# Joining the diagonal products of two token tiles into one planned operation in an encoder layer

## The chip, the cores and the metric

The kernel runs on one core of a Trainium2 chip. The metric is the device time of one execution in microseconds (us); lower is better. The engines are called TensorE (PE, with its weight loads as PEld), VectorE (DVE), ScalarE (ACT), GpSimd (POOL) and SyncE (SP, which here issues transfers).

## The reference

One layer of a bidirectional hybrid encoder on 512 tokens of width 1024, float32. One input projection feeds neighbourhood attention, a bidirectional state-space mixer (SSD) with 32 heads of width 64 in 8 groups, and gates; the branches are projected, merged and projected again, and a feed-forward layer follows. What matters here is the SSD mixer, which works in chunks of 128 tokens:

```python
def ssd_chunked(xh, dt, a, bmat, cmat):
    # xh (B,S,G,R,P), dt (B,S,G,R), a (G,R), bmat/cmat (B,S,G,N)
    ...
    a_cs = jnp.cumsum(adt, axis=-1)
    seg = a_cs[..., :, None] - a_cs[..., None, :]
    lmat = jnp.exp(jnp.where(tril, seg, -jnp.inf))
    cb = jnp.einsum('bclgn,bcsgn->bcgls', cc, bc)
    y_diag = jnp.einsum('bcgls,bcgrls,bcsgrp->bclgrp', cb, lmat, xc)
    states = jnp.einsum('bclgn,bcgrl,bclgrp->bcgrpn', bc, decay_states, xc)
    ...
    y_off = jnp.einsum('bclgn,bcgrpn,bcgrl->bclgrp', cc, prev, jnp.exp(a_cs))
    return (y_diag + y_off).reshape(bsz, s, g, r, p)
...
y_f = ssd_chunked(xs, dt[:, :, 0], a[0], bm, cm)
y_b = flip(ssd_chunked(flip(xs), flip(dt[:, :, 1]), a[1], flip(bm), flip(cm)))
y = y_f + y_b + xs * d_skip.astype(f32).reshape(SSD_GROUPS, HEADS_PER_GROUP)[..., None]
...
y = y * lax.rsqrt(jnp.mean(jnp.square(y), axis=-1, keepdims=True) + RMS_EPS)
y = y * ssd_norm_w.astype(f32).reshape(SSD_GROUPS, NORM_GROUP)
ys = y.reshape(bsz, s, D_INNER).astype(u.dtype) @ w_ssd_br
```

The change concerns `y_diag`, the products inside a chunk.

## The kernel before, in words

The first 485 us hold the input projection, the eight SSD groups and the projection of the SSD branch. Their instructions are not issued as the code is written: every step is first noted as an operation of a `Plan`, with its engine, a cost in us, the tile parts that it reads and writes, and whether it may fill gaps (`filler`, the long projections). A list scheduler then gives an order. The rank of an operation is its longest path to the end; `NUDGES`, a table of seeds and spreads, multiplies the ranks by small random factors, so each table gives another order. The start is written out by hand (`HEAD`, about the first 350 instructions of TensorE, to 58.9 us). `issue()` (L344) puts the hand-written start and the scheduled rest together, and `MOVE` there shifts one named operation ahead of another. Each engine then works its own queue in that order, and waits only for what its next instruction needs. Everything after the groups (attention, merge, feed-forward) has its order from the code.

For each group g, `ssd_project` makes four banks `ps_x` (B, C and two halves of x) by split products: `mm3` (L404 to L406) multiplies high times high, low times high and high times low parts, each 512 wide. `conv` copies each bank with a bias and a scale on ACT (L776), adds four taps on DVE (L784) and applies silu on ACT (L787), giving tiles `cv`. `z_project` makes `ps_z` the same way, 256 wide, and `sz` from it (L831). The weights of all of these come in slabs (`ws`), of which ACT makes the high half `wh` (L509) and POOL or DVE the low one `wl` (L513).

`ssd(g, ...)` then does, per group:

- `tp_b` (L858, transposes of B, which need `cv` of the first bank), `cb` (L868, the products of C and B, four token tiles in one bank), `tp_x` (L878) and `xtok` (L881), the weighted inputs `xw` (POOL, L913/L918), the chunk states `st` (L929, L941) and the states `hst`.
- For each half `c2` of the group, that is two token tiles `c`: one bank `yd` with room for both tiles. For each tile, a transfer brings the cumulated decays from DRAM (`acs_d`) to a tile `bc` (issued by SP at L959; there are 4 `bc` buffers). DVE and POOL subtract (L963), DVE makes a predicated copy (L967), ACT takes the exponent (L969), DVE multiplies by `cb` (L971). Then `f_yd` (L978) makes the diagonal products of that tile, 4 heads times 2 row halves, 64x64 each, which the profile shows as 16 instructions of form 128*64. So each half has two operations `f_yd`, each waiting for one `bc` and writing one half of the bank, and the planner may put them apart.
- `yo` (L993), the products across chunks, `t1`, `t2` and the sum `yz` (L1013).

`gated_norm(g, ...)` multiplies by `sz`, takes the sum of squares (ACT, L1028), finds the inverse root by 16 small operations on POOL (L1038 to L1056), scales the four tiles on ACT (L1059), and transposes on TensorE: two `tp_y` (L1075), from which ACT makes `yTh` (L1078) and DVE `yTl` (L1080). `ssd_branch` multiplies them by the slab `sbr` into eight banks `ps_sbr`, which are added up in `ysacc` (L1101; a copy for group 0).

Of the kernel before, what the change touches and what calls it, by code (L numbers as in the profile page):

```python
# [27 lines left out]
HD = 64  # L28
# [34 lines left out]

NUDGES = ((265225, 0.01), (410045, 0.001), (566648, 0.0005), (745606, 0.0005), (658272, 0.001), (17203, 0.0005),
          (943025, 0.0005), (429358, 0.001), (235890, 0.0005), (366213, 0.001))
LN0_BANKS = (("tr", "tr", "yd", "so"), ("tr", "tr", "yd", "tr"))
WDT = ("DVE", 0.66)
W0_ENG = lambda nc: (nc.gpsimd, nc.vector, nc.gpsimd, nc.vector)
# [36 lines left out]

MOVE = (("bc0_3.1", 2), ("bc0_2.0", 1))


class Plan:
# [233 lines left out]
    def issue(self):  # L343
        order = self.order(NUDGES)  # L344
        named = {}
        for o in self.ops:
            named.setdefault(".".join(map(str, o["w"][0])), []).append(o["i"])
        early, late = (named[x][n] for x, n in MOVE)
        head = [named[x[2:]].pop(0) for x in HEAD]
        order.remove(early)  # L350
        order.insert(order.index(late), early)
        done = set(head)
        for i in head + [i for i in order if i not in done]:
            self.ops[i]["fn"]()
# [3 lines left out]
def encoder_layer(ctx, tc, x, w_in, w_attn_br, w_ssd_br, w_o, w_ff1, w_ff2, pcols, rows64,  # L358
                  d_skip, ln_rows, rpb_pad, consts, lmask, out, dbg=None):
    nc = tc.nc  # L360
# [124 lines left out]
    op = plan.op  # L485

    def bank(name, tag, shape):
        return plan.tile(name, tag, psx, shape, F32)
# [36 lines left out]
    def load_x(t):  # L525
# [7 lines left out]
       r=[(xts[0].name, 0)], w=[(xts[2].name, 0), ("behind", 0)])  # L533
# [11 lines left out]
    for t in range(NT):  # L545
        for j in range(2):
# [3 lines left out]
           w=[("mv", t)])  # L550
# [298 lines left out]
    def ssd(g, bT, cT, x0, x1):  # L849
# [104 lines left out]
        for c2 in range(2):  # L954
            cs = slice(2 * c2, 2 * c2 + 2)
            yd = bank(f"yd{g}_{c2}", "yd", [P, 2, 256])
            for c in (2 * c2, 2 * c2 + 1):
                bc = local(f"bc{g}_{c}", "bc", [P, 2, HPG, P])
# [15 lines left out]

                def f_yd(c=c, bc=bc, yd=yd):
                    for h in range(HPG):
                        for rows in (slice(0, 64), slice(64, P)):
                            nc.tensor.matmul(yd()[rows, c % 2, h * HD : (h + 1) * HD],  # L978
                                             bc()[:, 1, h, rows],
                                             xtok()[:, c, h * HD : (h + 1) * HD], start=True, stop=True)  # L980
                op("PE", 0.9, f_yd, r=[(bc.name, 1), (xtok.name, c2)], w=[(yd.name, c % 2)])


# [828 lines left out]
```

## Time and profile before

| what | value |
| --- | --- |
| device time, median of 3 runs | 1178.44 us (1177.24 to 1178.65) |
| device time of the profiled execution | 1177.95 us |
| its span in the trace | 1176.2 us |
| mean granted clock of TensorE | 0.996 |
| busy time of TensorE | 1153.0 us, 98% of the span |

A row of the timeline reads: start in us, duration in us, engine, line, operation, the tile written and the tiles read, the shape, and the number of like instructions in a row; in square brackets the idle time of the engine just before, and what ended it. The start is that of the first of the row, the duration reaches to the end of the last. The matmuls overlap: each starts before the one ahead has ended, so their cost is read from start to start. Waits are given per line as total, number and longest.

### The profile page before, as it was taken

The page shows a single profiled execution, that of the slowest core. Times are in us where ns is not written, and L with a number is a line of the kernel's source. Part 1 is how long each engine was busy: PE and PEld are TensorE (multiplying, and loading weights), DVE is VectorE, ACT ScalarE, POOL GpSimd, SP SyncE. Part 2 cuts the span into 40 slices and gives each one's busy share as a digit, 9 for nine tenths or more (in the row PEclk, how much of TensorE's full clock was granted, in tenths as well). Part 3 has the DMA queues.
Part 4 walks back from the last instruction along what each step waited for, and adds up shares of the span by engine and source line. Part 5 has one row for each costly group of instructions (what it writes and reads, how often), then busy time and mean ns, then how long its engine had stood idle before and what let it go on. Part 6 is the DMA issues. An engine that isn't in the chain of part 4 may idle for free.

```text
span 1176.2 us, 16965 instructions
## 1 busy us (share of the span) xinstructions
PE 1153.0 (98%) x6394; PEld 977.1 (83%) x6394; DVE 765.4 (65%) x1363; ACT 614.9 (52%) x1033; POOL 545.5 (46%) x588
## 2 busy tenths in 40 slices
PE   5999999999999999999999999999999999999997
PEld 5988797879888888888888888888988888888886
DVE  7757476776766665434788975556543567498855
ACT  6677583836365554524667774342363554365410
POOL 1269968778788777204667630016046131221000
PEclk9999999999999999999999999999999999999999
DMA  6353333333333341233333313543236987888411
GB/s 202 98 161 124 108 126 108 125 106 129 108 108 111 123 144 59 85 108 86 93 78 89 77 47 108 179 156 131 73 108 192 239 202 189 188 214 224 151 65 54
DMA packets 129409, 149.22 MB, mean 127 GB/s; under 512 B 22960, under 2 KB 101808, under 8 KB 129328
## 3 DMA queue, kind: packets, MB, share of 16 engines
q1 hardware_dynamic: 115696, 112.63, 30.6%
q0 software_dynamic: 13056, 34.61, 12.2%
q8 instruction: 50, 0.82, 0.3%
q10 hardware_dynamic: 576, 0.92, 0.2%
q14 instruction: 31, 0.25, 0.1%
HBM read 145.90 MB, written 2.23 MB: 126 GB/s over the span
## 4 chain that ended last, share of the span: by engine, by line
PE 84%; DVE 5%; DMA 5%; issue 2%; ACT 2%; POOL 1%; SPq 1%; DVEq 0%; POOLq 0%; ACTq 0%
PE ps_f L404 8%; PE ps_f L406 8%; PE ps_f L405 8%; PE ps_x L404 4%; PE ps_x L406 4%; PE ps_x L405 4%; PE ps_abr L1370 4%; PE ps_z L404 3%; PE ps_z L405 3%; PE ps_z L406 3%; PE ps_sbr L404 2%; PE ps_sbr L406 2%; PE ps_sbr L405 2%; DMA w2r<-in_w_ff 2%; PE ps_g L405 2%; PE ps_g L404 2%
## 5 line engine op out<-in xcount | busy, mean ns | idle before, releaser
L784 DVE SCALAR_TENSOR_TENSOR cv<-ps_x,pc,cv 128x511 f32<-128x511 f32 (+1 forms) x128 | 95.7, 748 | 25.2 <-ACT cv L776 21.8
L405 PE MATMUL ps_f<-h1Th,wl_f 128*128 128x512 f32 (+1 forms) x288 | 104.1, 365 | 0.0
L404 PE MATMUL ps_f<-h1Th,wh_f 128*128 128x512 f32 (+1 forms) x288 | 103.6, 365 | 0.0
L406 PE MATMUL ps_f<-h1Tl,wh_f 128*128 128x512 f32 (+1 forms) x288 | 102.0, 365 | 0.0
L1573 DVE TENSOR_TENSOR wl_f<-w2r,wh_f 128x1024 fp32r<-128x1024 f32 x42 | 50.0, 1222 | 63.6 <-ACT wh_f L1572 63.3
L404 PE MATMUL ps_z<-wh_z,hTh 128*128 128x256 f32 x256 | 75.2, 294 | 0.0
L406 PE MATMUL ps_z<-wl_z,hTh 128*128 128x256 f32 x256 | 71.5, 279 | 0.0
L405 PE MATMUL ps_z<-wh_z,hTl 128*128 128x256 f32 x256 | 71.5, 279 | 0.0
L1567 POOL DMA_DIRECT2D w2r<-in_w_ff x30 | 36.3, 1415 | 72.5 <-DMA w2r<-in_w_ff 46.8
L405 PE MATMUL ps_f<-wh_f,sql 128*128 128x512 f32 x168 | 65.3, 390 | 0.0
L406 PE MATMUL ps_f<-wl_f,sqh 128*128 128x512 f32 x168 | 65.2, 390 | 0.1
L404 PE MATMUL ps_f<-wh_f,sqh 128*128 128x512 f32 x168 | 64.9, 389 | 0.0
L1572 ACT ACTIVATE wh_f<-w2r 128x1024 fp32r<-128x1024 f32 x42 | 42.7, 1054 | 42.0 <-DMA w2r<-in_w_ff 32.7
L1101 DVE TENSOR_TENSOR ysacc<-ps_sbr,ysacc 128x512 f32<-128x512 f32 x56 | 38.5, 689 | 37.5 <-PE ps_sbr L406 37.1
L404 PEld LDWEIGHTS ps_f<-h1Th,wh_f 128*128 128x128 f32 x288 | 53.9, 188 | 8.9
L405 PEld LDWEIGHTS ps_f<-h1Th,wl_f 128*128 128x128 f32 x288 | 53.9, 188 | 8.7
L406 PEld LDWEIGHTS ps_f<-h1Tl,wh_f 128*128 128x128 f32 x288 | 52.8, 188 | 8.7
L387 DVE TENSOR_TENSOR wl_f<-ws_f,wh_f 128x1024 fp32r<-128x1024 f32 x36 | 47.2, 1348 | 19.4 <-ACT wh_f L386 18.9
L404 PE MATMUL ps_x<-hTh,wh_bc 128*128 128x512 f32 (+1 forms) x144 | 56.6, 393 | 0.0
L404 PE MATMUL ps_sbr<-yTh,wh_sbr 128*128 128x512 f32 x128 | 55.8, 436 | 0.8 <-ACT yTh L1078 0.4
L406 PE MATMUL ps_x<-hTl,wh_bc 128*128 128x512 f32 (+1 forms) x144 | 53.5, 371 | 1.8 <-DVE hTl L626 1.8
L404 PE MATMUL ps_x<-hTh,wh_x 128*128 128x512 f32 (+1 forms) x144 | 54.6, 379 | 0.0
(344 smaller groups left out, 3717.0 us busy)
## 6 DMA issues: line engine op xcount, KB each, us to landing
ws_f<-in_w_ff SPq DMA_DIRECT2D x20, 1024.0 KB
w2r<-in_w_ff POOLq DMA_DIRECT2D x18, 1024.0 KB, 8.2
bc<-acs_d SPq DMA_DIRECT2D x32, 512.0 KB
w2r<-in_w_ff POOLq DMA_DIRECT2D x30, 512.0 KB, 8.9
ws_bc<-in_w_in SPq DMA_DIRECT2D x16, 512.0 KB
ws_x<-in_w_in SPq DMA_DIRECT2D x8, 1024.0 KB
ws_z<-in_w_in SPq DMA_DIRECT2D x8, 1024.0 KB
ws_g<-in_w_in SPq DMA_DIRECT2D x8, 1024.0 KB
```

What stands on the lines that cost most here:

```text
L387: (eng[i] if isinstance(eng, tuple) else eng).tensor_tensor(out=lo[:, k], in0=st[:, k], in1=hi[:, k].bitcast(F32), op=ALU.subtract)
L404: nc.tensor.matmul(o, lh, rh, start=start, stop=False)
L405: nc.tensor.matmul(o, ll, rh, start=False, stop=False)
L406: return nc.tensor.matmul(o, lh, rl, start=False, stop=stop)
L784: op("DVE", 0.75, lambda j=j, o=o, n=n: nc.vector.scalar_tensor_tensor(out=acc()[:, o], in0=ps()[:, n], scalar=tap(j), in1=acc()[:, o], op ...
L1101: op("DVE", 0.69, lambda d=d, ps=ps: nc.vector.tensor_tensor(out=ysacc[:, d, :], in0=ps(), in1=ysacc[:, d, :], op=ALU.add), r=[(ps.name, 0 ...
L1370: ins.append(nc.tensor.matmul(pss[j], u, v, start=k + p == 0, stop=k == KD - 1 and p == 2))
L1567: nc.gpsimd.dma_start(t, rows(i, n, c, k), accum_op=ALU.add)
L1572: nc.scalar.activation(hi[:, k], x, AF.Copy)
L1573: low = nc.vector.tensor_tensor(out=lo[:, k], in0=x, in1=hi[:, k].bitcast(F32), op=ALU.subtract)
```

## The change

The two `f_yd` of a half group become one operation. It is noted after both `bc` tiles are, with a cost of 1.2 us (`YD`) for the planner in place of two of 0.9, it reads both `bc` tiles and writes both halves of the bank. Its 16 matmuls of the program (32 in the profile) are the same ones in the same order as before within each tile. `MOVE` is dropped, with its use in `issue()`, and `NUDGES` is another table, of 14 entries in place of 10.

```diff
-NUDGES = ((265225, 0.01), (410045, 0.001), (566648, 0.0005), (745606, 0.0005), (658272, 0.001), (17203, 0.0005),
...
+NUDGES = ((169262, 0.0005), (921561, 0.003), (234225, 0.0005), (601575, 0.003), (892301, 0.001), (966086, 0.001), (247218, 0.001), (170282, 0.0005), (136193, 0.0005), (519613, 0.003), (845123, 0.0005), (776131, 0.001),
...
+YD = 1.2
...
-MOVE = (("bc0_3.1", 2), ("bc0_2.0", 1))
...
-        early, late = (named[x][n] for x, n in MOVE)
         head = [named[x[2:]].pop(0) for x in HEAD]
-        order.remove(early)
-        order.insert(order.index(late), early)
...
             yd = bank(f"yd{g}_{c2}", "yd", [P, 2, 256])
+            bcs = []
             for c in (2 * c2, 2 * c2 + 1):
                 bc = local(f"bc{g}_{c}", "bc", [P, 2, HPG, P])
...
-                def f_yd(c=c, bc=bc, yd=yd):
+                bcs.append(bc)
+
+            def f_yd(c2=c2, bcs=bcs, yd=yd):
+                for j, bc in enumerate(bcs):
                     for h in range(HPG):
                         for rows in (slice(0, 64), slice(64, P)):
-                            nc.tensor.matmul(yd()[rows, c % 2, h * HD : (h + 1) * HD],
-                                             bc()[:, 1, h, rows],
-                                             xtok()[:, c, h * HD : (h + 1) * HD], start=True, stop=True)
-                op("PE", 0.9, f_yd, r=[(bc.name, 1), (xtok.name, c2)], w=[(yd.name, c % 2)])
+                            nc.tensor.matmul(yd()[rows, j, h * HD : (h + 1) * HD], bc()[:, 1, h, rows],
+                                             xtok()[:, 2 * c2 + j, h * HD : (h + 1) * HD], start=True,
+                                             stop=True)
+            op("PE", YD, f_yd, r=[(bc.name, 1) for bc in bcs] + [(xtok.name, c2)],
+               w=[(yd.name, 0), (yd.name, 1)])
```

With the new table the whole order between 59 and 480 us is another one. The number of instructions on each engine is the same. Three places show how it differs; the numbers behind a name are the group, the tile or half, and a running number of the tile.

The first is TensorE in group 7, the second half of the diagonal products, before:

```order
L406 MATMUL ps_z7_1_4415<-wl_z7_4253,hTh_69 128x256
L978 MATMUL yd7_1_4447<-xtok7_4436,bc7_3_4143 64x64 x8
L929 MATMUL st7_03_4458<-xw7_3_4445,btok7_4259 128x256
L929 MATMUL st7_03_4458<-xw7_0_4456,btok7_4259 128x256
L978 MATMUL yd7_1_4447<-xtok7_4436,bc7_2_4133 64x64 x8
L404 MATMUL ps_z7_1_4415<-wh_z7_4238,hTh_69 128x256
```

And the same place now, TensorE in group 7:

```order
L404 MATMUL ps_z7_1_4415<-wl_z7_4252,hTh_69 128x256
L980 MATMUL yd7_1_4465<-xtok7_4454,bc7_2_4127 64x64 x8
L980 MATMUL yd7_1_4465<-xtok7_4454,bc7_3_3970 64x64 x8
L927 MATMUL st7_03_4486<-xw7_0_4482,btok7_4258 128x256
L927 MATMUL st7_03_4486<-xw7_3_4463,btok7_4258 128x256
L402 MATMUL ps_z7_1_4415<-wh_z7_4237,hTh_69 128x256
```

The two tiles now stand together, ahead of the `st` products that stood between them. Groups 3, 4 and 6 each had one half that was split in the same way; in group 0 and group 1 one half each had its two tiles far apart.

The second place is the end of group 0 on TensorE, where its transposes `tp_y0` meet the branch products `ps_sbr0`, before:

```order
L406 MATMUL ps_z1_1_1214<-wl_z1_1033,hTh_69 128x256
L1075 MATMUL tp_y0_1_1319<-cst_81,yz0_1093 128x128 x4
L1075 MATMUL tp_y0_0_1326<-cst_81,yz0_1093 128x128 x4
L929 MATMUL st1_03_1333<-xw1_0_1315,btok1_991 128x256
L929 MATMUL st1_03_1333<-xw1_3_1331,btok1_991 128x256
L404 MATMUL ps_sbr0_0_1347<-yTh0_1336,wh_sbr0_1154 128x512
```

On TensorE the same place now reads:

```order
L404 MATMUL ps_z1_1_1212<-wl_z1_1078,hTh_69 128x256
L1077 MATMUL tp_y0_0_1304<-cst_81,yz0_998 128x128 x4
L1077 MATMUL tp_y0_1_1309<-cst_81,yz0_998 128x128 x4
L402 MATMUL ps_sbr0_0_1329<-yTh0_1318,wh_sbr0_1230 128x512
L403 MATMUL ps_sbr0_0_1329<-yTh0_1318,wl_sbr0_1284 128x512
```

The two `st` products of group 1 no longer stand between the transposes and the branch products, and the transposes have changed places. ACT at the same place, from the scaling of `yz0` on, before:

```order
L1059 ACTIVATE yz0_1093<-yz0_1093,rs_y0_1234 128x256 x4
L509 ACTIVATE wh_bc2_1324<-ws_bc2_702 128x1024
L1078 ACTIVATE yTh0_1336<-tp_y0_1_1319,pc_83 128x512
L1078 ACTIVATE yTh0_1336<-tp_y0_0_1326,pc_83 128x512
L831 ACTIVATE sz1_1222<-ps_z1_1_1214 128x512
L509 ACTIVATE wh_bc2_1324<-ws_bc2_702 128x1024
```

ACT there now:

```order
L1061 ACTIVATE yz0_998<-yz0_998,rs_y0_1204 128x256 x4
L829 ACTIVATE sz1_1264<-ps_z1_1_1212 128x512
L507 ACTIVATE wh_bc2_1315<-ws_bc2_709 128x1024
L1080 ACTIVATE yTh0_1318<-tp_y0_0_1304,pc_83 128x512
L1080 ACTIVATE yTh0_1318<-tp_y0_1_1309,pc_83 128x512
L507 ACTIVATE wh_bc2_1315<-ws_bc2_709 128x1024
```

The `sz1` of the last `ps_z1` bank has moved ahead of both `yTh0`, and ahead of the half slab.

The third place is DVE in group 7, ahead of the taps of its first convolution `cv7_0`, before:

```order
L1013 TENSOR_TENSOR yz6_4101<-yd6_1_4112,t2_6_1_3977 128x256 x2
L963 TENSOR_TENSOR bc7_2_4133<-bc7_2_4133,amd_103 128x512
L963 TENSOR_TENSOR bc7_3_4143<-bc7_3_4143,amd_103 128x512
L784 SCALAR_TENSOR_TENSOR cv7_0_4179<-ps_x7_0_4139,pc_83,cv7_0_4179 128x510
L784 SCALAR_TENSOR_TENSOR cv7_0_4179<-ps_x7_0_4139,pc_83,cv7_0_4179 128x511 x2
```

DVE there now:

```order
L1015 TENSOR_TENSOR yz6_4083<-yd6_1_4104,t2_6_1_3966 128x256 x2
L1103 TENSOR_TENSOR ysacc_71<-ps_sbr5_7_4097,ysacc_71 128x512
L962 TENSOR_TENSOR bc7_1_4125<-bc7_1_4125,amd_103 128x512
L966 COPY_PREDICATED bc7_0_3972<-msk_100,bc7_0_3972 128x512
L782 SCALAR_TENSOR_TENSOR cv7_0_4177<-ps_x7_0_4133,pc_83,cv7_0_4177 128x510
L782 SCALAR_TENSOR_TENSOR cv7_0_4177<-ps_x7_0_4133,pc_83,cv7_0_4177 128x511 x2
```

Ahead of the taps stood the subtractions of two `bc` tiles; now one subtraction, of another tile, and one predicated copy stand there.

More of the change, by code (lines that the diff above doesn't have):

```diff
@@ L60 @@
 CC_N = 896
-NUDGES = ((265225, 0.01), (410045, 0.001), (566648, 0.0005), (745606, 0.0005), (658272, 0.001), (17203, 0.0005),
-          (943025, 0.0005), (429358, 0.001), (235890, 0.0005), (366213, 0.001))
+NUDGES = ((169262, 0.0005), (921561, 0.003), (234225, 0.0005), (601575, 0.003), (892301, 0.001), (966086, 0.001), (247218, 0.001), (170282, 0.0005), (136193, 0.0005), (519613, 0.003), (845123, 0.0005), (776131, 0.001),
+          (355392, 0.001),
+          (307293, 0.0005))
 LN0_BANKS = (("tr", "tr", "yd", "so"), ("tr", "tr", "yd", "tr"))
+YD = 1.2
 WDT = ("DVE", 0.66)
```

## The prediction

> **What bounds the kernel now.** I read the chain of work that ended last first, then the stage that the planner orders (59 to 485 us), then TensorE's waits in it. From the page's part 4, the chain's shares by engine:
>
> ```profile
> PE 84%; DVE 5%; DMA 5%; issue 2%; ACT 2%; POOL 1%; SPq 1%; DVEq 0%; POOLq 0%; ACTq 0%
> ```
>
> TensorE carries it, by far. The busy time by stretches (start and end, length, then PE, PEld, DVE, ACT, POOL, and the granted clock), for 59 to 485 us:
>
> ```profile
> 59.00:485.00 426.00, 424.47 (x2690) 357.48 (x2691) 272.14 (x441) 249.75 (x374) 333.69 (x346) 1.00 0.36 116
> ```
>
> TensorE is busy 424.47 of 426.00 us at full clock; POOL, the next of the others, 333.69. The waits of PE between 70 and 470 us:
>
> ```profile
> PE ps_sbr L404 <- ACT yTh L1078: 0.4, 1, 0.4
> PE tp_b L858 <- ACT cv L787: 0.4, 1, 0.4
> PE yd L978 <- DVE bc L971: 0.2, 1, 0.2
> ```
>
> One microsecond in three places. So this stage lasts as long as TensorE's own queue, and the change can act in two ways only: it alters what the queue itself costs, or it makes waits come or go. Outside the stage the instruction order is the same in both programs (up to 58.9 us, and from the last group's `tp_y` at about 480 us on), and I cost that at nothing: its cover is that the same instructions start from the same state.
>
> **The change, part by part. First, the merged product.** The count of instructions stays; what changes is how the diagonal products (`yd`) stand in TensorE's queue. Before, the 32 half-bank operations form 22 unbroken runs: of 16 pairs ten stand together, four are split by two `st` products, two lie far apart. After, there are 16 runs. What does a run cost by itself? One tile alone, then two together, each between products 512 wide (start, duration, engine, line, operation):
>
> ```profile
> 138.66 0.39 PE L405 MATMUL ps_x<-hTh,wl_bc 128*128 128x512 f32 x1
> 138.89 0.39 PE L406 MATMUL ps_x<-hTl,wh_bc 128*128 128x512 f32 x1
> 139.20 0.69 PE L978 MATMUL yd<-xtok,bc 128*64 128x64 f32 x16
> ...
> 140.38 0.40 PE L406 MATMUL ps_x<-hTl,wh_bc 128*128 128x512 f32 x1
> ```
> ```profile
> 415.40 0.39 PE L406 MATMUL ps_sbr<-yTl,wh_sbr 128*128 128x512 f32 x1
> 415.72 1.15 PE L978 MATMUL yd<-xtok,bc 128*64 128x64 f32 x32
> ...
> 417.36 0.40 PE L406 MATMUL ps_x<-hTl,wh_bc 128*128 128x512 f32 x1
> ```
>
> In steady work a 512-wide product takes one step of 0.23 us (138.66 to 138.89). From the last product ahead of the run to the third behind it, three steps are the products' own, 0.69. One tile: 140.38 − 138.89 − 0.69 = 0.80. Two together: 417.36 − 415.40 − 0.69 = 1.27. Two apart cost 1.60, so a joined pair saves 0.33. A pair that was split by `st`:
>
> ```profile
> 449.66 0.69 PE L978 MATMUL yd<-xtok,bc 128*64 128x64 f32 x16
> 450.28 1.13 PE L929 MATMUL st<-xw,btok 128*128 128x256 f32 x4
> 451.34 0.69 PE L978 MATMUL yd<-xtok,bc 128*64 128x64 f32 x16
> 451.95 0.39 PE L404 MATMUL ps_z<-wh_z,hTh 128*128 128x256 f32 x1
> ```
>
> It lasts 451.95 − 449.66 = 2.29. Joined, it is the 32 in 1.08 (the next product's 416.80 less 415.72; that row is the one left out above) and the `st` for at most the 1.06 that they take here, 2.14: at least 0.15 saved, and 0.33 if the `st` also loses a switch. I take 0.33 for all six, **−2.0**; the bounds are 2 × 0.33 + 4 × 0.15 = 1.3 and 2.0. The ten pairs that already stood together gain nothing, so the work of 16 merges is six merges' worth.
>
> The Trainium skill, "TensorEngine Tiling (Array Packing)", section "Key Properties", says that a change of the tiling mode, not of the tile alone, drains TensorE. The `yd` rows are 128*64 among 128*128, and the trace agrees that entry to and exit from a run cost something, 0.33 us; by that rule too the adjacent ten gain nothing.
>
> **Second, the waits that the new order moves.** *End of group 0.* Before, PE, then ACT:
>
> ```profile
> 119.51 1.03 PE L1075 MATMUL tp_y<-cst,yz 128*128 128x128 f32 x8
> 120.38 1.03 PE L929 MATMUL st<-xw,btok 128*128 128x256 f32 x4
> 121.85 0.50 PE L404 MATMUL ps_sbr<-yTh,wh_sbr 128*128 128x512 f32 x1 [0.44 <-ACT yTh L1078]
> 122.19 0.40 PE L405 MATMUL ps_sbr<-yTh,wl_sbr 128*128 128x512 f32 x1
> 122.72 0.50 PE L406 MATMUL ps_sbr<-yTl,wh_sbr 128*128 128x512 f32 x1
> ```
> ```profile
> 119.59 1.06 ACT L509 ACTIVATE wh_bc<-ws_bc 128x1024 fp32r<-128x1024 f32 x1 [1.29 <-PE ps_z L405]
> 120.55 1.25 ACT L1078 ACTIVATE yTh<-tp_y,pc 128x512 fp32r<-128x512 f32 x2
> 121.69 0.60 ACT L831 ACTIVATE sz<-ps_z 128x512 f32<-128x512 f32 x1
> ```
>
> The two `st` lay between the transposes and `ps_sbr` and covered part of the time in which ACT makes `yTh`; still about 0.9 is lost (0.44 in brackets, and the L406 product that waits for `yTl` comes 0.53 behind L405 instead of 0.23, with some delay left in the first step). After, `ps_sbr` stands right behind the transposes, and `sz` and half of `wh_bc` stand ahead of `yTh` on ACT. PE is ready at 119.51 + 0.87 (the step to 120.38) = 120.38. ACT starts `sz` at 119.59 (when `wh_bc` starts before), takes 0.60 for it, 0.96 for the slab half (119.59 to 120.55), and half of the 1.25 for the first `yTh`: 121.8. So PE waits 1.4 for it, and I estimate 0.2 for `yTl`, less than the 0.3 of before since its transpose is done earlier: 1.6 against 0.9, **+0.7**. Bounds: 0, if `sz` finds its bank ready early, and 1.2, if the slab half is late.
>
> *Group 7, ahead of `tp_b`.* DVE and PE before:
>
> ```profile
> 420.23 3.79 DVE L963 TENSOR_TENSOR bc<-bc,amd 128x512 f32<-128x512 f32 x2 [2.56 <-DMA bc<-acs_d]
> 423.94 3.09 DVE L784 SCALAR_TENSOR_TENSOR cv<-ps_x,pc,cv 128x510 f32<-128x510 f32 x4
> ```
> ```profile
> 428.26 0.39 PE L406 MATMUL ps_x<-hTl,wh_x 128*128 128x512 f32 x1
> 429.09 0.66 PE L858 MATMUL tp_b<-cst,cv 128*128 128x128 f32 x4 [0.44 <-ACT cv L787]
> ```
>
> Two subtractions that waited 2.56 for their transfer and took 3.79 hold up the taps of `cv7_0`, whose result `tp_b` waits for. The step from 428.26 is 0.83 instead of 0.23. After, one subtraction and one predicated copy stand there, and their transfers were issued a buffer earlier: the hold-up of 3.79 shrinks to about 2, more than the 0.6 lost. **−0.6** (bounds 0 and −0.6).
>
> *Group 0's first products.* Before, one half-bank operation waits:
>
> ```profile
> 83.94 0.69 PE L978 MATMUL yd<-xtok,bc 128*64 128x64 f32 x16 [0.24 <-DVE bc L971]
> ```
>
> With its steps 0.3; that place is gone, **−0.3**. In its stead stands a whole merged product, `yd0_0`, with a wait for both `bc` tiles, of which `bc0_0` is the last of five transfers. Behind it on PE are the `ps_x` products, ready long since. SP's issues (the slab `ws_x` behind them, at 68.20), the chain's transfer, and on DVE the first and the last step of such tiles, before:
>
> ```profile
> 66.35 1.81 SPq L959 DMA_DIRECT2D bc<-acs_d  x4
> ```
> ```profile
> 68.20 10.99 DMA ws_x<-in_w_in
> ```
> ```profile
> 70.33 0.69 DVE L963 TENSOR_TENSOR bc<-bc,amd 128x512 f32<-128x512 f32 x1 [7.13 <-DMA bc<-acs_d]
> ```
> ```profile
> 75.81 0.68 DVE L971 TENSOR_TENSOR bc<-bc,cb 128x512 f32<-128x512 f32 x1
> ```
>
> The five were in by 79.19, 12.8 after the first issue at 66.35. The slab now goes ahead of the four, and the first may go out as late as 68.2: the last lands between 79.2 and 81.0. A tile takes up to 76.49 − 70.33 = 6.2 with its queues; without them I estimate 4. So `yd0_0` is ready between 83.2 and 87.2; by the steps of the products ahead of it PE arrives at about 86.5. Wait 0 to 0.7, I take **+0.2**, nearer to the row that ends earlier.
>
> *Group 1's transposes.* A subtraction of `bc2_3` now stands on POOL ahead of the gated norm, and its transfer goes out only when `yd1_1` frees the buffer. In group 7 that hand-over took 420.23 − 415.72 = 4.5 us, and the norm and its scalings:
>
> ```profile
> 469.14 0.23 POOL L1038 TENSOR_SCALAR ssq<-ssq 128x4 f32<-128x4 f32 x1 [1.03 <-ACT sz L1028]
> ```
> ```profile
> 475.37 1.69 ACT L1059 ACTIVATE yz<-yz,rs_y 128x256 f32<-128x256 f32 x4
> ```
>
> or some 6.2 without the slab work between (4.5 of small operations, 1.69). With a subtraction of 1.1 to 1.9 that is 11 to 13, against about 12.5 of products on PE: 0 to 0.6, **+0.2**. All other groups keep their room by the same reckoning; the closest is under the rivals.
>
> **Sum:** −2.0 + 0.7 − 0.6 − 0.3 + 0.2 + 0.2 = −1.8 us in the stage. The profiled execution's own time was 1177.95 (span 1176.2), so 1176.1 by it; the median of the three runs shown is 1178.44, 0.5 above, so 1176.6 by the median. I take the median's, **1176.5**.
>
> **The rivals.** *The new order hides everything (B).* Every wait of the stage goes, the run costs go too: −2.0 and the 0.9, 0.6 and 0.3 above, with some 0.5 of small steps: −4.3, **1174.2**. For it: the waits are few and short. Against: ACT's order at the end of group 0 reads worse.
>
> *The scalings come late in groups 3 to 6 (C), the slower side.* These four groups have one and the same order. There the last two scalings of the norm stand on ACT behind the convolution's first step for the fourth `ps_x` bank, and `tp_y` follows that bank on PE after 18 products of `ps_z`. Those are 256 wide and take 18 × 0.12 = 2.1 us:
>
> ```profile
> 449.33 0.28 PE L405 MATMUL ps_z<-wh_z,hTl 128*128 128x256 f32 x1
> 449.45 0.28 PE L406 MATMUL ps_z<-wl_z,hTh 128*128 128x256 f32 x1
> ```
> ```profile
> 422.57 0.78 ACT L776 ACTIVATE cv<-ps_x,pc 128x512 f32<-128x512 f32 x1 [3.89 <-PE ps_x L406]
> ```
>
> ACT needs 0.78 and half of the 1.69, 1.6 in all, and some 0.2 in hand-overs: 0.3 to spare. If POOL's small operations end x later than the bank does, each of the four groups waits x − 0.3. At x = 0.8 the gain is gone; from x = 1.4 the kernel is slower by over 0.2%; at 1.5 it is 4 × 1.2 = 4.8 above the forecast, **1181.3**. For it: POOL is the fullest engine behind PE here (333.69 of 426), and one order serves four times. Against: no `tp_y` appears among the waits of before.
>
> *The change doesn't do what it says (D).* The entry cost of a run lies beside the weight loads, and only waits move: +0.7 − 0.6 − 0.3 + 0.4 = +0.2, or **1178.6**. For it: the durations of products are modelled. Against: 0.33 is taken from starts, not ends, and no other row between is late.
>
> The Trainium skill, "Perfetto Trace Analysis", section "Identifying the Most-Contended Engine", says that matmul busy time does not measure how close TensorE is to its limit and that the share of weight loads does. By that share, 357.48 of 426.00 or 84%, TensorE would have slack and D would be likelier; against it stands that products follow each other here at even steps with one microsecond of waits, so I leave D small.
>
> **How the numbers follow.** A, the sum with its terms at either end: 1175.3 to 1177.7, chance 0.48. B 0.20. C 0.18. D 0.14. Differences under 0.2%, or 2.4 us, are about what a measurement of this kernel can tell from no change: faster means below 1176.1, slower above 1180.8. A third of A lies below 1176.1: faster 0.16 + 0.20 = 0.36. Of C, x under 1.4 is still within: slower 0.14. Same: 0.50. The range takes in B down to 1173.6 and most of C, up to 1181.0.
>
> **What would show it.** In the changed profile: one run of 32 `yd` per half group, and from the product ahead to the third behind it 1.96; a bracket of about 1.3 on the first `ps_sbr`; no wait on `tp_b` of group 7; the `yd0_0` wait under 0.7. Waits on `tp_y` in groups 3 to 6, repeated at equal places, would be C. Equal run costs for 16 and 32 less their own products would leave D. A difference that arises outside 59 to 485 us would make the whole reckoning wrong.

## The result and the profile after

The changed kernel is slower: 1185.26 us median of 6 runs (1183.75 to 1189.36) against 1178.26 us (1177.24 to 1179.25, 6 runs) before, ratio 1.0068 with a 95% interval of 1.0057 to 1.0079. The forecast was 1176.5, so even its sign was wrong. The profiled execution is one of the two longest: 1189.28 us, span 1187.5. Between the same two products of TensorE (a hand-ordered `ps_z` at 56.36 us and a `ps_sbr` of the last group at 491.62 us in the old trace), the stage takes 446.21 us instead of 435.26, that is 10.95 more. What lies ahead of it is 0.6 us shorter, what lies behind it 1.0 us longer. The place is right, then, and the sum inside it is not.

The busy time by stretches for 59 to 485 us of the changed kernel (start and end, length, then PE, PEld, DVE, ACT, POOL, and the granted clock):

```profile
59.00:485.00 426.00, 415.43 (x2639) 351.28 (x2638) 268.43 (x438) 238.23 (x359) 321.22 (x339) 0.99 0.35 114
```

TensorE was busy 424.47 of these 426 us before. It idles now, and its waits between 60 and 490 us say where:

```profile
PE tp_x L876 <- DVE yTl L1082: 2.3, 1, 2.3
PE yd L980 <- DVE bc L970: 2.0, 1, 2.0
PE yo L995 <- DVE hst L946: 1.7, 1, 1.7
PE ps_sbr L402 <- ACT yTh L1080: 1.3, 1, 1.3
PE yo L995 <- DVE t L1007: 1.2, 1, 1.2
PE ps_x L402 <- DVE cv L782: 0.7, 1, 0.7
PE ps_z L402 <- DVE cv L782: 0.6, 1, 0.6
PE tp_b L856 <- ACT cv L785: 0.6, 2, 0.3
```

10.4 us against 1.0 before, and six of the eight rows name DVE. The first place in time is the first merged product, `yd0_0`. PE there, then DVE, then POOL:

```profile
88.75 1.15 PE L980 MATMUL yd<-xtok,bc 128*64 128x64 f32 x32 [2.02 <-DVE bc L970]
89.83 0.69 PE L402 MATMUL ps_x<-hTh,wh_bc 128*128 128x512 f32 x1
90.32 0.63 PE L403 MATMUL ps_x<-hTh,wl_bc 128*128 128x512 f32 x1
```
```profile
82.41 2.94 DVE L966 COPY_PREDICATED bc<-msk,bc 128x512 f32<-128x512 int32 x1
85.24 2.85 DVE L962 TENSOR_TENSOR bc<-bc,amd 128x512 f32<-128x512 f32 x1
```
```profile
81.90 5.65 POOL L511 TENSOR_TENSOR wl_x<-ws_x,wh_x 128x1024 fp32r<-128x1024 f32 x2
```

The predicated copy takes 2.94 us and the subtraction 2.85. The shortest of each in the same trace take 0.72 and 0.68. They are long while POOL makes the low half of a weight slab, `wl_x`, from 81.90 to 87.55, in two operations of which the second starts at 84.71: the copy ends 0.6 us behind the first, the subtraction 0.5 us behind the second. The product of `bc0_0` stands behind both on DVE, and `yd0_0` behind it. The second place, `tp_x` of group 2, has the same form. DVE, then POOL, then PE:

```profile
171.60 4.95 DVE L962 TENSOR_TENSOR bc<-bc,amd 128x512 f32<-128x512 f32 x2
176.65 1.38 DVE L966 COPY_PREDICATED bc<-msk,bc 128x512 f32<-128x512 int32 x1
177.93 1.39 DVE L1082 SCALAR_TENSOR_TENSOR yTl<-tp_y,pc,yTh 128x512 fp32r<-128x512 f32 x2
```
```profile
170.77 5.22 POOL L511 TENSOR_TENSOR wl_sbr<-ws_sbr,wh_sbr 128x1024 fp32r<-128x1024 f32 x2
```
```profile
178.71 1.97 PE L876 MATMUL tp_x<-cst,cv 128*128 128x128 f32 x8 [2.33 <-DVE yTl L1082]
```

Two subtractions, 4.95 instead of 1.4, beside `wl_sbr`; behind them `yTl`, which must free the bank that `tp_x` needs.

A second loss follows two of the waits. Behind `yd0_0` a 512-wide product takes a step of 0.43 us (90.32 to the next at 90.74) instead of 0.23. The stretches show the clock, in the column behind POOL:

```profile
88.00:90.00 2.00, 1.25 (x33) 1.19 (x34) 1.96 (x4) 0.00 (x0) 1.92 (x3) 0.99 0.00 0
90.00:92.00 2.00, 2.00 (x5) 1.55 (x6) 1.93 (x5) 0.21 (x1) 0.18 (x1) 0.50 0.72 168
92.00:93.00 1.00, 1.00 (x4) 0.78 (x3) 0.70 (x3) 1.00 (x1) 0.88 (x2) 0.50 0.93 258
93.00:95.00 2.00, 2.00 (x10) 1.59 (x9) 1.03 (x2) 0.70 (x2) 1.64 (x2) 0.90 1.01 388
```

The granted clock is 0.50 for some 3.4 us, which costs 1.7 us, and the same comes behind the wait of 2.33 at `tp_x`. The Trainium skill, "TensorE: Matmul & The Clock Gate", section "What's actually happening", puts the half clock behind an idle window of about 3.4 us, of a free-running count; this trace has it behind waits of 2.02 and 2.33 us, and the measurement decides.

**The account of the profiled execution.** The steps lost at waits in its stage (brackets and the delay around them) sum to 12.3 us, the half clock to 3.4. Before, the same steps sum to 2.9. The merged runs save an estimated 2.1 us, six times the 0.35 measured below on one of them. So 12.3 + 3.4 − 2.9 − 2.1 = 10.7, against 10.95 measured. The median of the runs lies 4.0 below this execution; two half clocks would be 3.4 of that, but no other run of this kernel has a trace.

One more view, DVE's groups with their mean in ns, after and then before:

```profile
L962 DVE TENSOR_TENSOR bc<-bc,amd 128x512 f32<-128x512 f32 x32 | 41.0, 1288 | 44.5 <-DMA bc<-acs_d 44.5
L966 DVE COPY_PREDICATED bc<-msk,bc 128x512 f32<-128x512 int32 x32 | 32.4, 1032 | 5.5 <-POOL bc L962 5.0
```
```profile
L963 DVE TENSOR_TENSOR bc<-bc,amd 128x512 f32<-128x512 f32 x32 | 37.9, 1194 | 21.0 <-DMA bc<-acs_d 20.7
L967 DVE COPY_PREDICATED bc<-msk,bc 128x512 f32<-128x512 int32 x32 | 36.0, 1156 | 0.5 <-POOL bc L963 0.3
```

73.4 us after and 73.9 before, where 32 of each at 0.69 and 0.75 would be 46. The old order lost as much in collisions. It lost it where TensorE had other work; the new one lost it in front of TensorE.

The kernel's own planner knows of such meetings. Its operations on DVE and POOL can carry a mark `lock`, and an operation so marked is not started in the plan while a marked one of the other engine runs. The `bc` subtraction, the predicated copy and the slab operation carry it; the product of `bc` and `cb` does not. The plan keeps them apart by planned times; on the chip each engine works its queue as its inputs arrive, and here they met.

### The profile page after: what moved, and what is told of

The parts are those of the page before. It is cut to its first block, busy times and chain, and to the rows that moved or that the text cites. A ratio compares the mean times of both kernels' runs of the same rounds, so it can differ in the third digit from the quotient of the medians.

```text
span 1187.5 us, 16958 instructions
## 1 busy us (share of the span) xinstructions
PE 1154.2 (97%) x6394; PEld 978.9 (82%) x6394; DVE 763.2 (64%) x1363; ACT 607.0 (51%) x1026; POOL 539.4 (45%) x588
## 4 chain that ended last, share of the span: by engine, by line
PE 77%; DVE 7%; DMA 7%; ACT 3%; POOL 3%; issue 3%; SPq 0%; DVEq 0%; POOLq 0%; ACTq 0%
PE ps_f L402 7%; PE ps_f L403 7%; PE ps_f L404 7%; PE ps_x L402 4%; DMA w2r<-in_w_ff 4%; PE ps_x L404 4%; PE ps_x L403 4%; PE ps_abr L1372 4%; PE ps_z L402 2%; PE ps_z L404 2%; PE ps_z L403 2%; PE ps_sbr L402 2%; PE ps_sbr L404 2%; PE ps_sbr L403 2%; PE ps_g L404 2%
## 5 line engine op out<-in xcount | busy, mean ns | idle before, releaser
L782 DVE SCALAR_TENSOR_TENSOR cv<-ps_x,pc,cv 128x510 f32<-128x510 f32 (+1 forms) x128 | 95.6, 749 | 31.7 <-ACT cv L774 28.0
L1569 POOL DMA_DIRECT2D w2r<-in_w_ff x30 | 36.3, 1417 | 73.9 <-DMA w2r<-in_w_ff 47.6
L962 DVE TENSOR_TENSOR bc<-bc,amd 128x512 f32<-128x512 f32 x32 | 41.0, 1288 | 44.5 <-DMA bc<-acs_d 44.5
L402 PE MATMUL ps_sbr<-yTh,wh_sbr 128*128 128x512 f32 x128 | 58.4, 456 | 1.4 <-ACT yTh L1080 1.3
```

Of the source, the lines that this page charges most:

```text
L402: nc.tensor.matmul(o, lh, rh, start=start, stop=False)
L782: op("DVE", 0.75, lambda j=j, o=o, n=n: nc.vector.scalar_tensor_tensor(out=acc()[:, o], in0=ps()[:, n], scalar=tap(j), in1=acc()[:, o], op ...
L962: op(e, us, lambda d=d, eng=eng, c=c, bc=bc: eng.tensor_tensor(out=bc()[:, d], in0=bc()[:, d], in1=by_dir(amd, c, g)[:, d, :].unsqueeze(2) ...
L1569: nc.gpsimd.dma_start(t, rows(i, n, c, k), accum_op=ALU.add)
```

## The experiments

The theory: a DVE operation that reads two tiles of the on-chip memory (the `bc` subtraction, the predicated copy) waits while a POOL slab operation runs, and the new order puts such meetings ahead of what TensorE needs next. The rivals: the merged operation waits for the later of two transfers; or the run costs of my first term are imagined. In the diffs a pair (a, b) moves operation a to just ahead of b in the issued order; `name#n` is the n-th planned operation that writes that part first. "Before" was timed anew with each set of runs.

**1. The old order with pairs joined.** Old `NUDGES` and `MOVE`; only these moves:

```diff
+SHIFT = (('yd0_1.1#0', 'yd0_1.0#0'), ('yd3_1.1#0', 'yd3_1.0#0'), ('yd4_1.1#0', 'yd4_1.0#0'),
+         ('yd6_0.1#0', 'yd6_0.0#0'), ('yd7_1.1#0', 'yd7_1.0#0'))
```

> The order of before, with five of the six separated pairs of diagonal products joined (the earlier operation moved to just ahead of the later one: group 0 second half, group 3 and 4 second half, group 6 first half, group 7 second half). Nothing else moves. If a run of diagonal products costs an entry of its own (the first term of the prediction, 0.33 us a pair, at least 0.15 for the split ones), this is 5 x 0.33 = 1.65 us faster than before, at least 0.9: about 1176.6 to 1177.4, ratio 0.9986 to 0.9992. If that term was imagined, no difference: ratio 1.0000. If joining by itself makes waits, slower than before by the wait, seen at one of the five places.

Measured: 1186.18 us (1181.31 to 1188.34), ratio 1.0058 [1.0042, 1.0074]; slower. The joining itself, in group 3: PE before (the last product ahead of the block, and the third behind it), then here:

```profile
231.87 0.28 PE L406 MATMUL ps_z<-wl_z,hTh 128*128 128x256 f32 x1
...
234.94 0.39 PE L406 MATMUL ps_sbr<-yTl,wh_sbr 128*128 128x512 f32 x1
```
```profile
231.08 0.28 PE L422 MATMUL ps_z<-wl_z,hTh 128*128 128x256 f32 x1
231.32 1.27 PE L945 MATMUL st<-xw,btok 128*128 128x256 f32 x4
232.52 1.15 PE L994 MATMUL yd<-xtok,bc 128*64 128x64 f32 x32
...
234.19 0.40 PE L422 MATMUL ps_sbr<-yTl,wh_sbr 128*128 128x512 f32 x1
```

3.07 us before and 3.11 here: a joined pair *behind* its `st` saves nothing. Groups 6 and 7 agree: from the block's first product to the third behind it 2.62 us each here, 2.64 before. `st` to `yd` costs 1.20 here (231.32 to 232.52), 1.06 before. In the changed kernel the pair stands *ahead* of its `st`:

```profile
238.56 1.15 PE L980 MATMUL yd<-xtok,bc 128*64 128x64 f32 x32
239.65 1.13 PE L927 MATMUL st<-xw,btok 128*128 128x256 f32 x4
240.43 0.47 PE L402 MATMUL ps_z<-wh_z,hTh 128*128 128x256 f32 x1
240.73 0.28 PE L403 MATMUL ps_z<-wh_z,hTl 128*128 128x256 f32 x1
240.85 0.28 PE L404 MATMUL ps_z<-wl_z,hTh 128*128 128x256 f32 x1
```

From the first `yd` to the third product behind the block it is 2.29 us. The split pair of the prediction started at 449.66, and its third product is this row of before:

```profile
452.30 0.28 PE L406 MATMUL ps_z<-wl_z,hTh 128*128 128x256 f32 x1
```

2.64 us: 0.35 saved. The first term holds, then, for the order that the change makes, and not for the one that I tried here. What made the profiled execution slower are new waits, 4.4 us in brackets against 1.0, of which two are of `ps_sbr` for `ysacc`, 2.8 us. The longer one is behind a collision. DVE, POOL and PE in group 6:

```profile
406.35 4.03 DVE L983 COPY_PREDICATED bc<-msk,bc 128x512 f32<-128x512 int32 x2
```
```profile
406.99 5.60 POOL L529 TENSOR_TENSOR wl_bc<-ws_bc,wh_bc 128x1024 fp32r<-128x1024 f32 x2
```
```profile
411.00 0.51 PE L420 MATMUL ps_sbr<-yTh,wh_sbr 128*128 128x512 f32 x1 [1.86 <-DVE ysacc L1117]
```

The same two copies took 1.81 in the old trace, where `wl_bc` began 1.2 us behind them instead of 0.6. The profile is of the fastest of this kernel's six runs; what the longer ones lost was not seen.

**2. One slab operation moved on POOL.**

```diff
+SHIFT = (('wl_x1.0#0', 't2_0_1.1#0'), ('wl_x1.1#0', 't2_0_1.1#0'))
```

> The changed kernel with one move: the two halves of the slab operation wl_x1 on POOL stand behind three small additions, so that they no longer run beside the predicated copy and the subtraction on DVE ahead of the first merged product yd0_0. Collision theory (a subtraction or predicated copy on DVE that meets a slab operation on POOL waits for it, 2.9 instead of 0.7 us, and holds up what TensorE needs): the copy and the subtraction fall to about 0.75 and 0.7 us, the wait of yd0_0 (2.0 us) goes, and with it the half clock that follows: 2 to 4 us less than the changed kernel, ratio to before 1.003 to 1.005. Joint-wait theory (the merged product waits for the later of its two transfers): the wait at yd0_0 stays at 2 us, ratio to before stays about 1.007.

Measured: 1183.73 us (1182.80 to 1184.83), ratio 1.0044 [1.0032, 1.0056]. That is 2.8 us less than the changed kernel by the two ratios, 2.0 by the medians, each against its own before. DVE and PE:

```profile
82.92 1.27 DVE L982 COPY_PREDICATED bc<-msk,bc 128x512 f32<-128x512 int32 x1
84.09 1.22 DVE L978 TENSOR_TENSOR bc<-bc,amd 128x512 f32<-128x512 f32 x1
```
```profile
87.65 1.15 PE L996 MATMUL yd<-xtok,bc 128*64 128x64 f32 x32
```

No bracket on `yd0_0`, and no half clock behind it. The copy and the subtraction did not fall to 0.75 and 0.7 as expected: they now run beside three small additions on POOL. DVE's queue and the transfers' were not touched, so neither the merged operation nor its transfers held it up.

**3. DVE's queue changed at three places.**

```diff
+SHIFT = (('bc2_2.0#1', 'coef2.0#0'), ('bc2_3.0#1', 'coef2.0#0'), ('bc2_3.0#2', 'coef2.0#0'),
+         ('bc2_3.1#1', 'bc2_2.0#2'), ('bc2_3.1#2', 'bc2_2.0#2'),
+         ('hst3.4#0', 'bc4_1.0#1'), ('t1_6_2.0#0', 'bc7_0.0#1'))
```

> The changed kernel with DVE's queue changed at three places: in group 2 two bc subtractions and a predicated copy (with the exponent and the product behind them) stand behind yTl1 instead of ahead of it; in group 3 one bc subtraction stands behind the first hst sum; in group 6 one stands behind t1 of tile 2. Collision theory: the waits of tp_x in group 2 (2.3 us), of yo in group 3 (1.7) and of yo in group 6 (1.2) go, and the half clock behind the first (about 1.6 us lost): 5.5 to 7.3 us less than the changed kernel, ratio to before 1.000 to 1.002. If the waits come from late transfers or from POOL alone, they stay or come back at the next instruction, and the ratio stays near 1.007.

Measured: 1182.96 us (1179.71 to 1183.59), ratio 1.0031 [1.0019, 1.0043], 4.4 us less than the changed kernel by the ratios (2.8 by the medians); more was expected. The waits of `tp_x` and of `yo` in groups 3 and 6 are gone, and the half clock of group 2 too. But one `yo` still waits 1.7 us for `hst`. It is the `yo` of group 5 now, at 352 us: the groups have one order, all of it is earlier, and a collision has come up in a later group. There the `bc` subtraction starts at 348.56, beside `wl_bc` from 348.54, and takes 2.91 us; in the changed kernel it started 0.23 us ahead of the slab and took 0.82.

**4. All five places.** Moves 2 and 3, and the end of group 0 as before:

```diff
+         ('sz1.1#0', 'wh_bc2.1#0'), ('xw1_3.0#0', 'wl_bc2.0#0'), ('xw1_0.0#0', 'wl_bc2.0#0'),
+         ('st1_03.1#0', 'ps_sbr0_0.0#0'), ('st1_03.0#0', 'ps_sbr0_0.0#0')
```

> The changed kernel with the moves of the two runs before, and the end of group 0 as it was before the change (the two st products of group 1 between the transposes and ps_sbr0, with their POOL inputs; sz1 behind yTh0 on ACT). Collision theory plus the run costs of the prediction: of the 12 us that TensorE waits for in the changed kernel some 2 us stay, so 9 to 13 us less than the changed kernel's profiled run, and a time below that of before: 1174 to 1177 us, ratio 0.997 to 0.999. If the gain of joined runs is imagined but the collisions are real: ratio about 1.000. If other waits take the place of those removed: above 1.002.

Measured: 1178.77 us (1176.60 to 1179.95), ratio 0.9997 [0.9988, 1.0005]. The whole loss is gone, the expected gain is not there: waits of 1.7 (`yo`, group 5), 0.9, 0.8, 0.7 and 0.3 us remain or are new. By its number alone this could also mean that the gain of joined runs is imagined; run 12 decides that.

**5 and 6. POOL's slab operations in quarters**, in the changed kernel and in the one before:

```diff
-                out=wl()[:, k], in0=ws()[:, k], in1=wh()[:, k].bitcast(F32), op=ALU.subtract),
...
+                for j in range(4):
...
+                    on.tensor_tensor(out=wl()[:, s[0], s[1]], in0=ws()[:, s[0], s[1]],
+                                     in1=wh()[:, s[0], s[1]].bitcast(F32), op=ALU.subtract)
```

> The changed kernel, its order untouched, but every slab operation on POOL that makes low weight parts (128x1024, 2.4 us) is cut into four of a quarter each inside the same planned step. Collision theory: a subtraction or predicated copy on DVE then waits for a quarter (0.6 to 0.7 us) instead of up to 2.2 us, so the waits of yd0_0, tp_x of group 2, yo of groups 3 and 6, ps_z of group 1 and ps_x of group 7 shrink to a third or vanish, and the half clock with them; those at the end of group 0 (1.3) and at tp_b stay: 6 to 10 us less than the changed kernel, ratio to before 0.999 to 1.002. Rival (POOL itself or late transfers hold TensorE up): the cut makes POOL's work some 5% longer, and the ratio is 1.007 or more.

> The kernel before, with the same cut of POOL's slab operations into quarters. Collision theory: its order was lucky, few collisions lie ahead of TensorE, so there is little to gain: up to 1.5 us of its 2.9 us of waits, ratio 0.9985 to 1.000. Rival (longer POOL work costs): 1.001 or more.

Measured: 1183.45 us, ratio 1.0049 [1.0036, 1.0062], and 1180.66 us, ratio 1.0016 [1.0007, 1.0025]. Mixed. In the changed kernel the slabs' subtractions on POOL are now busy for 184 us instead of 151, which I had put at 5% more and is 22%. Of the six waits aimed at five are gone and the `yo` of group 3 waits 0.8 us, but `yo` waits for `hst` three times in all, 3.6 us. In the old kernel the rival's bound came true (1.001 or more): new waits of 0.8, 0.6, 0.6 and 0.5 us stand there. In the changed kernel the longest copy stood beside no slab at all. DVE, then POOL's row of operations (first and last of four rows that follow each other without a gap):

```profile
128.77 5.57 DVE L989 COPY_PREDICATED bc<-msk,bc 128x512 f32<-128x512 int32 x1 [6.41 <-POOL bc L985]
```
```profile
128.70 2.04 POOL L934 TENSOR_TENSOR xw<-xtok,wst 128x512 f32<-128x512 f32 x2
...
132.70 1.04 POOL L1010 TENSOR_TENSOR t<-xtok,coef 128x512 f32<-128x512 f32 x1
```

It came 0.07 us late and, by these rows, waited for five POOL operations in a row.

**7. Joined pairs and quarters together.** The moves of 1 and the edit of 6.

> The kernel of the first run (order of before, five pairs joined) with the quarters. It was 0.58% slower than before, by my reading of its profile not because of the joining but because it shifted POOL's slab operations onto DVE's copies in groups 4 and 6 (ps_sbr waits for ysacc, 2.8 us), more of it in the runs that were not profiled. Collision theory: with quarters these waits are gone and the 5 x 0.33 us of saved entries show: ratio to before 0.997 to 0.999, and 0.9985 against the uncut order of before with quarters. If joining costs by itself (both transfers must be in): still above 1.002.

Measured: 1183.29 us (median of six runs, 1180.67 to 1183.99 and one of 2351.77 that the ratio leaves out), ratio 1.0039 [1.0025, 1.0052]. The expected gain failed, and the number is the one put down for a cost of joining. `ps_sbr`'s waits for `ysacc` are gone, but the pairs' gain was not to be had (run 1 says why), and POOL is late in five places (`st` waits for `xw`, 2.0 us; 0.5 in run 1). It tells little more.

**8. The merged operation alone**, with the old table and the old `MOVE`:

> The merged operation alone: the old table of nudges and the old MOVE, the planner's cost 1.2. This is a third order. If the merge itself is what costs, the ratio is again about 1.007. If the loss belongs to the order and comes from chance collisions, the ratio can be anything from 0.998 to 1.015, and its waits stand at other instructions than in the changed kernel, each behind a subtraction or copy on DVE of over 1.5 us that runs beside a slab operation.

Measured: 1195.29 us (1194.33 to 1197.54), ratio 1.0150 [1.0134, 1.0166]. The old order with this operation in it changes part of what is computed; which part was not looked for, so the time is a hint only. Its longest wait, 4.3 us, is of `tp_y` for ACT, at no place where the changed kernel waits. Around it the granted clock is 0.50 for some 10 us. My expectation that each wait stands behind a collision failed here: ahead of that scaling ACT has a table load and two halves of `wh_bc`. So this run shows that another order has other waits, not that collisions make them, and an old table does not carry over to a plan with another operation in it.

**9 and 10. POOL's slab operations without reads**: three fillings with zero (0.96 us each) in place of each subtraction, in the changed kernel and in the one before. The low parts of these weights are left out.

```diff
-                out=wl()[:, k], in0=ws()[:, k], in1=wh()[:, k].bitcast(F32), op=ALU.subtract),
...
+                for j in range(3):
+                    nc.gpsimd.memset(wl()[:, k].bitcast(F32), 0.0)
```

> The changed kernel with POOL's slab operations (low weight parts) replaced by three fillings with zero of the same tiles, so that they read nothing; the low parts of these weights are left out of the result. Order, transfers and all else as they were. Collision theory: subtractions and copies on DVE no longer wait for the slabs (none over 1.8 us), and of the waits in the stage only those at the end of group 0 (1.3 us) and small ones stay: 8 us or more less than the changed kernel, 1174 to 1177 us, ratio to before 0.996 to 0.999. If the waits come from the merged operation or from transfers they stay, and the ratio stays above 1.004.

> The kernel before with the same replacement (the low parts left out). Both programs without the slabs' reads show what the merge and the new order are worth without collisions: by the first term of the prediction the changed one is then 2.0 us faster than this one, less 0.7 for the end of group 0, so 1 to 2 us. This one against before: its few waits (2.9 us) shrink, ratio 0.998 to 1.000. If the saved entries are imagined, the two are equal or the changed one is slower.

Measured: 1178.88 us, ratio 1.0003 [0.9994, 1.0012], and 1178.82 us, ratio 1.0006 [0.9998, 1.0015]. The first is the decisive run: the new order and its merged products untouched, POOL busy even longer (2.9 instead of 2.45 us a half), and the loss of 0.68% is gone, though the time is 2 us above the range that I had given. Its waits:

```profile
PE ps_sbr L418 <- ACT yTh L1101: 1.3, 1, 1.3
PE tp_b L877 <- ACT cv L806: 1.0, 1, 1.0
PE st L948 <- POOL xw L937: 0.5, 1, 0.5
PE ps_x L418 <- DVE cv L803: 0.3, 1, 0.3
```

All DVE waits but 0.3 us have left. The subtractions and the copies on DVE, whose means were 1288 and 1032 ns in the changed kernel:

```profile
L983 DVE TENSOR_TENSOR bc<-bc,amd 128x512 f32<-128x512 f32 x32 | 24.0, 758 | 44.1 <-DMA bc<-acs_d 44.1
L987 DVE COPY_PREDICATED bc<-msk,bc 128x512 f32<-128x512 int32 x32 | 26.9, 863 | 7.3 <-POOL bc L983 6.7
```

One thing more changed here: a filling does not read `wh`, so POOL no longer waits for ACT ahead of it (96 us in all in the changed kernel), and the fillings start at other times. That alone does not explain the result, since the operations still meet: of the subtractions that stand alone in the timeline, 14 run beside a filling and take 1.17 us at most, where 13 beside the slabs of the changed kernel take up to 2.88. The Trainium skill, "SBUF — State Buffer", section "Who interferes with whom", says that a DVE instruction with two SBUF inputs contends with a GpSimd instruction that reads SBUF, not with one that only writes it; its section "Summary: rules for kernel authors" adds that the second one to issue blocks until the first finishes. The fillings agree, and so does `bc` times `cb`, where `cb` lies in PSUM (0.69 at the longest, in the old kernel also beside the slabs). The copy of run 5, which waited for five operations and not for one, does not agree. The expectation of run 10 failed: 9 is not 1 to 2 us faster than 10. Its stage is 0.75 us shorter (434.93 against 435.68), because 9 still waits 3.1 us and 10 waits 1.3.

**11 and 12. More moves.** Run 11 is run 4 with the first `hst` sum ahead of the next subtraction in groups 4 and 5 too, and two copies behind the taps of `cv1_2`:

```diff
+         ('hst4.4#0', 'bc5_0.0#1'), ('hst5.4#0', 'bc6_0.0#1'),
+         ('bc0_2.0#2', 'wl_z1.1#0'), ('bc1_1.0#2', 'wl_z1.1#0')
```

Run 12 is run 11, changed for the waits that this left:

```diff
-         ('bc0_2.0#2', 'wl_z1.1#0'),
-         ('xw1_3.0#0', 'wl_bc2.0#0'), ('xw1_0.0#0', 'wl_bc2.0#0'),
+         ('xw1_3.0#0', 'wl_sbr0.1#0'), ('xw1_0.0#0', 'wl_sbr0.1#0'),
+         ('bc7_0.0#2', 'cv7_0.0#5'), ('bc7_0.1#1', 'cv7_0.0#5')
```

> The changed kernel with all moves of the fourth run and more of them on DVE: the first hst sum ahead of the next group's subtraction in groups 4 and 5 too, and two copies of group 0 and 1 behind the taps of cv1_2. Of that run's remaining waits the yo of group 5 (1.7 us) and ps_z of group 1 (0.8) go: 2 to 3 us less than it, 1175.5 to 1177 us, ratio 0.9975 to 0.999. If the removed waits come back elsewhere: ratio 0.9995 to 1.001 again.

> The changed kernel with the moves of the last run, less one and with two more, for the waits that it still had: only one copy (bc1_1) stands behind the taps of cv1_2, the POOL inputs of group 1's st stand ahead of the second half of wl_sbr0, and in group 7 a copy and its exponent stand behind the taps of cv7_0. The waits of yd0_1 (1.2 us), st (1.1) and ps_x of group 7 (0.7) go: 2 to 3 us less than that run, 1174.7 to 1176 us, ratio to before 0.997 to 0.9985, the first to be clearly below before. If every removed wait is followed by another, as collision by chance would have it: ratio 0.999 to 1.001.

Measured: run 11 1177.70 us, ratio 0.9996 [0.9987, 1.0004], with the removed waits replaced by one of 1.2 at `yd0_1`, so the expected gain did not come; run 12 1175.34 us (1173.76 to 1176.51, 11 runs) against 1178.06, ratio **0.9976 [0.9967, 0.9985]**, faster than both kernels and as expected. Its stage and all its waits between 60 and 490 us:

```profile
59.00:485.00 426.00, 425.17 (x2702) 359.83 (x2702) 264.04 (x442) 247.17 (x372) 327.47 (x346) 1.00 0.36 116
```
```profile
PE tp_b L872 <- ACT cv L801: 0.5, 1, 0.5
```

The stage takes 432.58 us, 2.7 less than before. An estimate of the shares: about 2.1 from the merged runs (six times 0.35), the rest from waits, whose brackets fell from 1.1 to 0.5.

## Why the prediction was wrong

- **What bounds the kernel:** right. The change acted through TensorE's queue and its waits only, inside the stage.
- **The merged product, −2.0:** right as a mechanism and in size for this order (0.35 measured for one split pair with `yd` ahead of `st`, 0.33 taken; the total of six is an estimate). Not for any joining: run 1 shows no saving with `st` ahead. My lower bound of 0.15 excluded that.
- **End of group 0, a wait of 1.6 in place of 0.9:** right. The bracket is 1.3, and with its steps 1.8.
- **Group 1's transposes, +0.2:** no wait of `tp_y` is on the list, so the term was nothing.
- **Group 7, −0.6:** wrong. `tp_b` still waits 0.3, and the `ps_x` ahead of it 0.7. The subtraction and the predicated copy ahead of the taps, which I put at about 2 us together, took 2.81 and 2.94 beside `wl_x`.
- **`yd0_0`, 0 to 0.7:** this is a step that failed. The tile's work was put at 4 to 6.2 us behind its transfer. DVE and POOL took the tile at 80.4, as reckoned (the transfer between 79.2 and 81.0), and the product was ready at 88.7: 8.3 us. The bound of 6.2 was one tile of the old order, and it held no full collision.
- **"All other groups keep their room by the same reckoning":** the step that failed most. The sum has no term for an operation that takes longer because of POOL. `tp_x`, the two `yo`, `ps_z` and `ps_x`, together 6.5 us of brackets, stand behind subtractions and copies of 2.3 to 2.95 us in place of 0.7. The rows were there to be read: the prediction quotes two subtractions at 3.79 us, where one takes 0.69 elsewhere, and calls it a hold-up without asking what POOL did (`wl_x` ran to 421.7).
- **The half clock** was not in the reckoning. It added 1.7 us to each of two waits of the profiled execution.
- **The ends of A** do not follow from the terms. With every term at its own bound the sum runs from −2.9 to +0.9 us, by the median from 1175.5 to 1179.3, not from 1175.3 to 1177.7. Even so the ends stay far below 1185.3.
- **The rivals:** C had the right kind (the slower side, one order used in four groups, POOL against another engine) and the wrong place: the `tp_y` waits that it named never came, and its mechanism, a late POOL chain, was not the one. B's list of waits that go was right for 0.3 of 1.8 us.

## What to carry to other kernels

When a change re-plans a stage whose bound engine is 99% busy, the saved work is small and the new waits can be larger: read durations of the same instruction against each other first, since a spread like the 0.7 to 2.9 us here can be a collision, and walk the new order with the long value wherever the other engine's work may overlap. A re-planned order is to be timed and then mended by its list of waits: here nineteen small moves turned +0.68% into −0.24%. Where a planner marks operations that must not meet, as `lock` does here, the marks name the candidates. Joining small products pays by the neighbours that are left, not by the count of operations.

## What the runs showed of the hardware

- One predicated copy that came 0.07 us behind a POOL operation waited, by its rows, for five of them, 5.57 us (run 5): DVE did not get a turn between them. In other places it did, between quarters of a slab (no copy that stands alone over 1.3 us beside them).
- The half clock, about 3.4 us at 0.50, came behind waits of 2.00, 2.02, 2.33 and 2.45 us (run 5, the changed kernel twice, run 2). It did not come behind 1.72, 1.86 and 1.87 (the changed kernel, runs 1 and 3), nor behind another of 2.45 in run 8. Near 14 us every profile has a wait of 1.66 to 1.85 us. The half clock follows all four of 1.84 or 1.85, among them the old kernel's (0.58 granted for 16 to 20 us), one of 1.72, and of the nine of 1.66 only that of run 3, not the changed kernel's (1.00). So one wait can have two prices. That this makes part of the spread from 1183.75 to 1189.36 us is argued, not shown, since only one of those runs has a trace.
